# Row-wise largest magnitude of an 8192 x 8192 matrix: 25 tail loads over an 18-row run, and the first load in eight transfers

## The chip, the cores and the metric

The kernel runs on one core of one Trainium2 chip. The metric is the device time of one execution in microseconds (us), the median of several runs. All stretches and instants below are from one profiled execution, and count from the start of its span.

## The reference

```python
def setup_inputs():
    return {
        "x": np.random.randn(8192, 8192).astype(np.float32),
    }

def reference(x: np.ndarray) -> np.ndarray:
    return np.linalg.norm(x, ord=np.inf, axis=1)
```

For a matrix and axis 1 this is the largest absolute value of each row: 268 MB are read, 32 KB are written, and each element is looked at once.

## The kernel before

**Layout.** SBUF holds one ring of 3 x 16384 float32 columns on 128 partitions (`RING`), and behind it a few columns more (`PAD`). Every load goes into the ring by a DMA that SyncE (SP) issues. `Pieces.room` gives out the ring's columns in turn and starts over when a load doesn't fit in what is left. VectorE (DVE) reduces each landed load by `tensor_reduce` with maximum and absolute value, to one column for each matrix row in it.

**The big part.** The first 8192 - 14 x 128 = 6400 rows are taken in 25 loads of two rows a partition: 128 x 16384 columns, 64 KB a partition, 8.389 MB each. In load t, partition p takes rows 256t + 2p and 256t + 2p + 1. One reduction a load writes two results a partition into `res_big`. When all are there, two TensorE transposes and two ScalarE copies turn them into `line`, of 25 rows, which one output DMA stores.

**The tail.** The last 14 x 128 rows (`ROWS = 14`) are laid out as one run of 14 matrix rows, 14 x 8192 columns, on each partition. `tail_loads` cuts this run into 23 loads, worked out from the end backwards: the last has 1344 columns (`FIRST`), and each one before it is as large as the cost of reducing and loading what follows allows. `LOAD` and `REDUCE` are the costs that it reckons with (us a column and us for each operation). `SNAP` moves a cut onto the start of a matrix row when it comes near one, `GRAIN` rounds sizes.

**Combining.** A row of the tail that lies in several loads has a partial result for each; GpSimd (POOL) takes the maximum of these (`tensor_scalar`, L207) into `res_tail`. The last row is treated in another way: its partial results stand directly behind the columns of the last load (`RING + k`), so that the last reduction takes them along. For that it waits until the reduction just ahead of it has written the last of them.

**Order and waits.** Each load has one of 8 semaphores (`SEMS`) in turn. A reduction waits for its load's semaphore; the further reductions of a load that spans several rows keep program order. SP issues all loads in program order from one queue. A load waits for the reductions that read the ring columns it overwrites, and for the reduction of the load 8 before it. The output DMA of `line` (L216) is issued after all input loads; the output of `res_tail`, after the last reduction (L220), ends the kernel.

The lines of the profile that matter: L82 the loads, L100 the reductions, L207 the combinations on POOL, L216 and L220 the two output DMAs.

Of the kernel before, what the change touches and what calls it, by code (L numbers as in the profile page):

```python
# [8 lines left out]
P = 128  # L9
R = 2  # L10
RING = 3 * 16384
PAD = 16
SEMS = 8


LOAD = (1.1775e-3, 0.075)
REDUCE = (1.0417e-3, 0.060)
ROWS = 14
FIRST = 1344
SNAP = 0.5  # L20
GRAIN = 64


def tail_loads(n_cols, big):

    slack = 0.0
    lag = REDUCE[0] * FIRST + REDUCE[1]
    loads = []
    left = ROWS * n_cols
    while left:
        room = lag + slack
        w = FIRST if not loads else 0
        n = 0
        while not w or (loads and n):

            n += 1
            start = (left - 1) // n_cols * n_cols - (n - 1) * n_cols
            fit = int((room - REDUCE[1] * n) / REDUCE[0])
            w = max(w, min(fit, left - start) // GRAIN * GRAIN)
            if fit <= left - start or start <= 0:
                break
        w = max(GRAIN, min(w, big, left))
        row = (left - w + n_cols - 1) // n_cols * n_cols
        if loads and left - row >= SNAP * w:
            w = left - row  # L50
        n = (left - 1) // n_cols - (left - w) // n_cols + 1
        slack += (LOAD[0] - REDUCE[0]) * w + LOAD[1] - REDUCE[1] * n
        loads.append(w)
        left -= w
    return loads[::-1]


class Pieces:
# [7 lines left out]
    def __init__(self, tc, ring):  # L66
        self.tc, self.nc, self.ring, self.head = tc, tc.nc, ring, 0
        self.sems = [tc.alloc_semaphore(f"loaded{i}") for i in range(SEMS)]
        self.started = self.reduced = 0
        self.last = []  # L70

    def room(self, w):
        if self.head + w > RING:
            self.head = 0
        at = self.head
        self.head += w
        return at

    def load(self, at, w, src):
        i = self.started  # L80
        self.started += 1
        ins = self.nc.sync.dma_start(out=self.ring[:, at : at + w], in_=src)  # L82
        ins.then_inc(self.sems[i % SEMS], 16)
        self.tc.no_tile_sem_insts.add(ins.ins.name)
        self.tc.declare_no_dep(ins.ins, group="loads", reason="a reduction stands in between")
        self.tc.add_to_no_dep_group("loads", ins.ins)
        if i >= SEMS:
            self.tc.add_manual_dep(
                ins.ins,
                self.last[i - SEMS].name,  # L90
                mybir.DependencyInfo(mybir.DependencyClass.Sync, mybir.DependencyReason.DATA),
                reason="the semaphore counts one load at a time",
            )

    def reduce(self, pairs):

        i = self.reduced
        self.reduced += 1
        for k, (dst, src) in enumerate(pairs):
            ins = self.nc.vector.tensor_reduce(  # L100
                out=dst,
                in_=src,
                axis=mybir.AxisListType.X,
                op=mybir.AluOpType.max,
                apply_absolute_value=True,
            )
            if k:
                self.tc.keep_in_program_order(ins)
            else:
                ins.wait_op(self.sems[i % SEMS], 16 * (i // SEMS + 1), "sem-ge")  # L110
            self.tc.declare_no_dep(ins.ins, group="loads", reason="waits on the load's semaphore")
        self.last.append(ins.ins)
        return ins


@with_exitstack
def kernel(
    ctx: ExitStack,
    tc: tile.TileContext,
    x: bass.AP,  # L120
    out: bass.AP,
):
    nc = tc.nc
    f32 = mybir.dt.float32
    n_rows, n_cols = x.shape

    tail = tail_loads(n_cols, R * n_cols)
    split = n_rows - ROWS * P
    n_big = split // (R * P)

    x_big = x[:split].rearrange("(t p r) m -> t p (r m)", p=P, r=R)
    x_tail = x[split:].rearrange("(p r) m -> p (r m)", p=P)

    single = ctx.enter_context(tc.tile_pool(name="single", bufs=1))
    psum_pool = ctx.enter_context(
        tc.tile_pool(name="psum", bufs=1, space=bass.MemoryType.PSUM)
    )
    ring = single.tile([P, RING + PAD], f32)  # L140
    ident = single.tile([P, P], f32)
    res_big = single.tile([P, n_big, R], f32)
    res_tail = single.tile([P, ROWS], f32)
    make_identity(nc, ident)
    pieces = Pieces(tc, ring)

    for t in range(n_big):
        at = pieces.room(R * n_cols)
        pieces.load(at, R * n_cols, x_big[t])
        buf = ring[:, at : at + R * n_cols]  # L150
        pieces.reduce([(res_big[:, t, :], buf.rearrange("p (r m) -> p r m", r=R))])


    line = single.tile([n_big, P, R], f32)
    for r in range(R):
        ps = psum_pool.tile([n_big, P], f32, name=f"ps{r}")
        nc.tensor.transpose(ps, res_big[:, :, r], ident)  # L157
        nc.scalar.copy(out=line[:, :, r], in_=ps)  # L158


    parts = []
    col = 0
    for i, w in enumerate(tail):
        c = 0
        while c < w:
            row = (col + c) // n_cols
            n = min(w - c, (row + 1) * n_cols - col - c)
            parts.append((row, i, c, n))
            c += n
        col += w  # L170
    of_row = [[q for q in parts if q[0] == row] for row in range(ROWS)]


    behind = len(of_row[-1]) - 1
    dst = {}
    for row, own in enumerate(of_row):
        if row == ROWS - 1:
            for k, q in enumerate(own[:-1]):
                dst[q] = ring[:, RING + k : RING + k + 1]
            dst[own[-1]] = res_tail[:, row : row + 1]  # L180
        elif len(own) == 1:
            dst[own[0]] = res_tail[:, row : row + 1]
        else:
            some = single.tile([P, len(own)], f32, name=f"parts{row}")
            for k, q in enumerate(own):
                dst[q] = some[:, k : k + 1]
    col = 0
    for i, w in enumerate(tail):
        final = i == len(tail) - 1
        at = RING - w if final else pieces.room(w)  # L190
        pieces.load(at, w, x_tail[:, col : col + w])
        col += w
        own = [q for q in parts if q[1] == i]
        done = pieces.reduce(
            [
                (dst[q], ring[:, at + q[2] : at + q[2] + q[3] + (behind if q == parts[-1] else 0)])
                for q in own
            ]
        )
        for row in range(ROWS - 1):  # L200
            if len(of_row[row]) > 1 and of_row[row][-1][1] == i:
                best = dst[of_row[row][0]]
                more = [dst[q] for q in of_row[row][1:]]
                while more:
                    two, more = more[:2], more[2:]
                    to = best if more else res_tail[:, row : row + 1]
                    nc.gpsimd.tensor_scalar(  # L207
                        out=to,
                        in0=best,
                        scalar1=two[0],  # L210
                        scalar2=two[1] if len(two) == 2 else None,
                        op0=mybir.AluOpType.max,
                        **(dict(op1=mybir.AluOpType.max) if len(two) == 2 else {}),
                    )
    tc.declare_fence(done.ins, group="loads")
    nc.sync.dma_start(  # L216
        out=out[:split].rearrange("(t q) -> t q", q=P * R),
        in_=line.rearrange("t p r -> t (p r)"),
    )
    nc.sync.dma_start(out=out[split:].rearrange("(p r) -> p r", p=P), in_=res_tail)  # L220
# [1 line left out]
_INS = ['x']  # L222
_OUTS = [((8192,), 'float32')]
# [25 lines left out]
```

## Time and profile before

| what | value |
|---|---|
| median of 3 runs | 630.21 us (629.86 to 630.43) |
| profiled execution | 629.88 us |
| its span | 628.0 us |
| VectorE busy | 551.6 us, 88% |
| DMA queue q1 | 268.47 MB in 7086 packets, 428 GB/s over the span |
| one reduction of 128x16384 | 17.22 us |
| one reduction of 128x8192 | 8.675 us |
| reduction of the last load (128x1348) | 1.557 us |
| first load, issue to landing | 21.9 us |
| later big loads, issue to landing | 40.8 us (median) |

The span is the time in which the program's instructions run; the execution's own time has 1.88 us around it. "Issue to landing" counts the time that a load stands in the queue behind others, and so says little on how long its bytes take; for that one compares landings. [...]The DMA share of a stretch counts packets by the moment at which they start, so that short stretches show bursts over 1.

### The profile page before, as it was taken

How to read it: one execution, taken by the hardware profiler on the slowest of the kernel's cores; microseconds unless marked ns; L12 is line 12 of the kernel's file. 1: busy time of each engine (PE TensorE's matmuls, PEld its weight loads, DVE VectorE, ACT ScalarE, POOL GpSimd, SP SyncE). 2: the span in 40 equal slices, each digit the busy share in tenths (PEclk: the TensorE clock that was granted, in tenths of full speed). 3: DMA queues.
4: the chain of work that ended last, by engine and by line, in shares of the span. 5: the costliest groups of instructions: out<-in, count | busy, mean ns of one | idle time of the engine just before them, and what ended most of it. 6: DMA issues, size and time to landing. Idle time of an engine off the chain costs nothing.

```text
span 628.0 us, 165 instructions
## 1 busy us (share of the span) xinstructions
PE 0.6 (0%) x2; PEld 0.2 (0%) x2; DVE 551.6 (88%) x51; ACT 1.8 (0%) x3; POOL 2.5 (0%) x12
## 2 busy tenths in 40 slices
PE   0000000000000000000000000000000000000000
PEld 0000000000000000000000000000000000000000
DVE  0588988889988889888898888998888999999998
ACT  0000000000000000000000000000000000000000
POOL 0000000000000000000000000000000000000000
DMA  9999999999999999999999999999999999999996
GB/s 401 405 463 401 468 401 468 401 468 401 468 401 468 401 468 401 468 401 468 401 468 401 468 401 468 401 468 401 468 401 434 434 430 434 413 434 433 426 424 281
DMA packets 7086, 268.47 MB, mean 428 GB/s; under 512 B 917, under 2 KB 942, under 8 KB 1582
## 3 DMA queue, kind: packets, MB, share of 16 engines
q1 hardware_dynamic: 7086, 268.47, 99.1%
HBM read 268.44 MB, written 0.03 MB: 428 GB/s over the span
## 4 chain that ended last, share of the span: by engine, by line
DMA 55%; DVE 44%; issue 0%; DVEq 0%
DMA ring<-in_x_dram 55%; DVE res_big L100 25%; DVE res_tail L100 10%; DVE parts L100 8%; DVE ring L100 1%; DVEq L100 0%
## 5 line engine op out<-in xcount | busy, mean ns | idle before, releaser
L100 DVE TENSOR_REDUCE res_big<-ring 128x2 f32<-128x16384 f32 x25 | 430.5, 17220 | 73.8 <-DMA ring<-in_x_dram 73.8
L100 DVE TENSOR_REDUCE res_tail<-ring 128x1 f32<-128x8192 f32 (+1 forms) x8 | 61.8, 7785 | 0.1
L100 DVE TENSOR_REDUCE parts<-ring 128x1 f32<-128x384 f32 (+13 forms) x14 | 52.1, 3799 | 0.0
L100 DVE TENSOR_REDUCE ring<-ring 128x1 f32<-128x1728 f32 (+2 forms) x4 | 7.5, 1925 | 0.0
L207 POOL TENSOR_SCALAR res_tail<-parts 128x1 f32<-128x1 f32 x6 | 1.8, 305 | 613.9 <-DVE parts L100 613.9
L158 ACT COPY line<-ps 25x128 f32<-25x128 f32 x2 | 0.5, 262 | 502.9 <-PE ps L157 502.9
L158 ACT ACT_TABLE_LOAD x1 | 1.3, 1283 | 0.7 <-PEq L233 0.7
L157 PE MATMUL ps<-ident,res_big 128*25 128x128 f32 x2 | 0.6, 399 | 504.5 <-DVE res_big L100 504.5
masks.py:199 POOL TENSOR_SCALAR_AFFINE_SELECT ident<-ident 128x128 f32<-128x128 f32 x1 | 0.3, 292 | 0.1
L157 PEld LDWEIGHTS ps<-ident,res_big 128*25 128x25 f32 x2 | 0.2, 123 | 504.4 <-issue 504.4
masks.py:197 POOL MEMSET ident<- 128x128 f32 x1 | 0.2, 204 | 0.3 <-POOLq L233 0.3
L233 POOL MEMSET const-bfloat16-1.0<- 128x1 bf16 x1 | 0.1, 102 | 0.0
L233 POOL MEMSET const-uint8-127<- 128x1 uint8 x1 | 0.1, 101 | 0.0
L233 POOL MEMSET const-float32-0.0<- 128x1 f32 x1 | 0.1, 98 | 0.2 <-issue 0.2
L233 POOL MEMSET const-float32-1.0<- 128x1 f32 x1 | 0.1, 98 | 0.0
## 6 DMA issues: line engine op xcount, KB each, us to landing
ring<-in_x_dram SPq DMA_DIRECT2D x6, 4096.0 KB, 35.9
ring<-in_x_dram SPq DMA_DIRECT2D x1, 4288.0 KB, 34.0
ring<-in_x_dram SPq DMA_DIRECT2D x1, 3904.0 KB, 42.9
ring<-in_x_dram SPq DMA_DIRECT2D x1, 3200.0 KB, 38.8
ring<-in_x_dram SPq DMA_DIRECT2D x1, 2848.0 KB, 45.2
ring<-in_x_dram SPq DMA_DIRECT2D x1, 2272.0 KB, 38.8
ring<-in_x_dram SPq DMA_DIRECT2D x1, 2144.0 KB, 39.8
ring<-in_x_dram SPq DMA_DIRECT2D x1, 2112.0 KB, 42.0
```

Source lines behind the costliest of these rows:

```text
L100: ins = self.nc.vector.tensor_reduce(out=dst, in_=src, axis=mybir.AxisListType.X, op=mybir.AluOpType.max, apply_absolute_value=True,)
L157: nc.tensor.transpose(ps, res_big[:, :, r], ident)
L158: nc.scalar.copy(out=line[:, :, r], in_=ps)
L207: nc.gpsimd.tensor_scalar(out=to, in0=best, scalar1=two[0], scalar2=two[1] if len(two) == 2 else None, op0=mybir.AluOpType.max, **(dict(op ...
L233: nc = _bacc.Bacc("TRN2", target_bir_lowering=False, num_devices=1)
```

## The change

- The tail's run has 18 matrix rows a partition instead of 14, and is cut into 25 loads instead of 23. Two big loads fewer are left (23), so the number of loads is 48 as before.
- `tail_loads` gives a start and a size for each load. The sizes come from the same costs, with `FIRST = 1152` and `SNAP = 0.7`. The very last load is still the end of the last row. The last but one is now the end of the row before it (1280 columns), and the four other pieces of the last row come ahead of that.
- The last load has columns of its own behind the ring (`APART`), with the partial results of its row behind them.
- The first load is issued as eight transfers of 16 partitions: transfer k takes partitions k, k + 8, ..., k + 120, and all eight count on the same semaphore. The first reduction waits for 8 x 16.
- Before the last output DMA, SP waits for POOL in a no-op of its own; the DMA then waits for VectorE only.

The loads of the tail in order, in columns:

```
before  8192 x6, 8576, 7808, 4288, 6400, 5696, 4224, 4544, 4032, 3584, 3008, 2752, 2432,
        1728, 1920, 1728, 1472, 1344
after   16384, 9600, 14976, 12736, 11840, 8192 x3, 5888, 6976, 6208, 5504, 3776, 4416, 3328,
        3520, 3072, 2752, 2432, 1984, 1920, 1664, 1472, 1280, 1152
```

The core of the diff:

```diff
-PAD = 16
+APART = 2048
-ROWS = 14
-FIRST = 1344
-SNAP = 0.5
+ROWS = 18
+FIRST = 1152
+SNAP = 0.7
...
+    ends = [take(end, end - n_cols, FIRST), take(end - n_cols, end - 2 * n_cols, n_cols)]
+    for top, bottom in zip(ends, (end - n_cols, 0)):
+        while top > bottom:
+            top = take(top, bottom, big)
     return loads[::-1]
...
-        ins = self.nc.sync.dma_start(out=self.ring[:, at : at + w], in_=src)
-        ins.then_inc(self.sems[i % SEMS], 16)
...
+        pairs = [(self.ring[:, at : at + w], src)]
+        if i == 0:
+            dst, src = (v.rearrange("(j k) c -> j k c", k=8) for v in pairs[0])
+            pairs = [(dst[:, k], src[:, k]) for k in range(8)]
+        for to, of in pairs:
+            ins = self.nc.sync.dma_start(out=to, in_=of)
+            ins.then_inc(self.sems[i % SEMS], 16)
+            self.counts[i % SEMS] += 16
...
+        self.due.append(self.counts[i % SEMS])
...
-                ins.wait_op(self.sems[i % SEMS], 16 * (i // SEMS + 1), "sem-ge")
+                ins.wait_op(self.sems[i % SEMS], self.due[i], "sem-ge")
...
+            spots[own[-1][1]] = at
+            at += own[-1][3]
+            for q in own[:-1]:
+                dst[q] = ring[:, at : at + 1]
+                at += 1
+            behind[own[-1]] = len(own) - 1
...
-        at = RING - w if final else pieces.room(w)
+        at = spots[i] if i in spots else pieces.room(w)
...
-    nc.sync.dma_start(out=out[split:].rearrange("(p r) -> p r", p=P), in_=res_tail)
+    seen = nc.sync.keepalive_nop([nc.sync.lower_ap(res_tail[:, ROWS - 2 : ROWS - 1])])
+    tc.keep_in_program_order(seen)
+    tc.no_tile_sem_insts.add(seen.ins.name)
+    tc.add_to_no_dep_group("seen", seen.ins)
+    last = nc.sync.dma_start(out=out[split:].rearrange("(p r) -> p r", p=P), in_=res_tail)
+    tc.declare_no_dep(last.ins, group="combined", reason="SyncE has waited for GpSimd")
+    tc.declare_fence(last.ins, group="seen")
```

`take(top, bottom, most)` cuts one load of at most `most` columns off the end of the columns from `bottom` to `top`, and returns where it starts.

## The prediction

> **What bounds the kernel now.** I read the page's busy times first, then the chain of waits, then the timeline of the end, then busy time by stretch. VectorE (DVE) is busy 88% of the span, yet the DMA row of the slices is full to the last but one: the stream of loads sets the time.
>
> ```profile
> PE 0.6 (0%) x2; PEld 0.2 (0%) x2; DVE 551.6 (88%) x51; ACT 1.8 (0%) x3; POOL 2.5 (0%) x12
> DMA  9999999999999999999999999999999999999996
> HBM read 268.44 MB, written 0.03 MB: 428 GB/s over the span
> ```
>
> The chain (start, length, what) says which one ends last where. Up to 487 every step is a load; then VectorE alone carries it.
>
> ```profile
> 0.72 21.94 DMA ring<-in_x_dram
> 22.68 17.23 DVE res_big L100
> 39.93 40.76 DMA ring<-in_x_dram
> ...
> 504.32 60.15 DVE res_tail L100 x7
> 564.47 52.04 DVE parts L100 x14
> 616.51 7.38 DVE ring L100 x4
> 623.89 0.03 issue
> 623.92 0.02 DVEq L100
> 623.94 0.05 issue
> 623.99 1.56 DVE res_tail L100
> ```
>
> The first big reduction starts at 22.68, the 25th at 487.10: (487.10 - 22.68)/24 = 19.35 us a load of 8.389 MB, or 433.5 GB/s, against 17.22 of reducing. So each microsecond by which the first load lands later moves everything behind it by as much.
>
> The start is the one stretch where the stream isn't full (columns: stretch, its length, busy of each engine, clock, DMA share, GB/s by when packets start):
>
> ```profile
> 0.00:1.73 1.73, 0.00 (x0) 0.00 (x0) 0.00 (x0) 1.01 (x1) 0.68 (x6) 1.00 0.00 0
> 1.73:2.10 0.37, 0.00 (x0) 0.00 (x0) 0.00 (x0) 0.27 (x1) 0.00 (x0) 1.00 5.80 1948
> 2.10:2.90 0.80, 0.00 (x0) 0.00 (x0) 0.00 (x0) 0.00 (x0) 0.00 (x0) 1.00 1.02 410
> 2.90:4.80 1.90, 0.00 (x0) 0.00 (x0) 0.00 (x0) 0.00 (x0) 0.00 (x0) 1.00 0.00 0
> 4.80:5.40 0.60, 0.00 (x0) 0.00 (x0) 0.00 (x0) 0.00 (x0) 0.00 (x0) 1.00 4.03 1748
> ```
>
> 1948 x 0.37 and 410 x 0.80 make 0.72 and 0.33 MB: 11 and 5 packets of 65,536 B, one for each of the 16 DMA engines, started over 1.17 us. Their second packets start between 4.8 and 5.4. At full rate a round of 16 takes 1.049 MB / 433.5 GB/s = 2.42 us, so the last engine could have been ready at 1.73 + 2.42 = 4.15 and was at 5.4: at most 1.25 us lies there.
>
> At the end the last load is issued at 607.82 (timeline of SP) and lands 15.9 later, at 623.7; its reduction starts at 623.99. The 0.27 between is VectorE's: busy until 623.89, then 0.10 for the wait on the reduction just before, whose result the last one reads.
>
> [...]reductions with no wait between them overlap by 0.08 us (one of 8192 lasts 8.675, seven take 60.15), and the one that waits for its neighbour starts 0.10 after it.
>
> **The change, part by part.**
>
> *First load.* Transfer k holds partitions k, k+8, ..., k+120. [...]38.5 us instead of 19.35: **+19.2**. [...]Below, nothing excludes 0[...]. Above, 2 x 19.35 gives +19.35.
>
> Nothing covers it: DVE has nothing before the first landing, and loads 2 and 3 are queued behind. Ring space can't give it back, since load 4 waits for the first reduction.
>
> *Start of the stream.* 16 descriptors in the first transfer instead of 128 may bring the engines in sooner: between 0 and -1.25. [...]I take **-0.2**.
>
> *Issues.* SP issues at 0.72, 1.16 and 1.63 before, some 0.45 apart; seven more move the second big load's issue from 1.16 to about 4.3, under a first load that lasts past 22: nothing. Each transfer also ends in a semaphore write. Between 487.08 (landing) and 623.7, 23 loads of 114,688 columns take 136.6 us; with 19.35 for 16384 that is 1.1765 ns a column and 0.073 us a load. The 0.073 holds its packets too, and these stay 128; seven times between 0 and 0.073 is 0 to +0.51: **+0.1**.
>
> *Tail.* 25 + 23 loads become 23 + 25, of the same bytes: the stream is as long as before. Reductions cost 1.0418 ns a column (8.675 for 8192 against 0.541 for 384) and start 0.06 further apart than that (60.15 / 7 = 8.593). Followed load by load from the last big landings, with the old start: VectorE waits 1.75 at the load of 14976 and is never idle again; the last three land at 620.68, 622.26 and 623.69 and start at 620.82, 622.41, 623.81. The ring never holds the stream up: every tail load is issued at least 13 us ahead of its turn. Before, the start was 623.99: -0.18. The new last but one (row 16) stands between the last reduction and the fourth part that it reads, so that wait is met. The last reduction is 1156 columns, not 1348: 192 x 1.0418 = -0.20. Sum **-0.38**; -0.47 if VectorE's lag of 0.10 isn't there, -0.2 if the wait isn't gone.
>
> *Behind it.* Row 16 needs two POOL operations after the reduction of 1280, which ends at 623.89: start 0.1 later as after 616.51 in the trace (616.62), 0.36 + 0.28 and 0.1 between gives 624.75; the last reduction ends at 623.81 + 1.36 = 625.17. So 0.4 of cover; were it gone, the excess would count in full. SP's no-op passes then, and only the output DMA waits for VectorE: before, 0.09 from 625.55 to its issue at 625.64; **-0.04** (0 to -0.07). The 23-row output on one engine: 23 packets of 1 KB[...]; 0.05 each is an upper bound from the 45 packets between 622.81 and 623.23; 1.2 us, done by 625, before the last output's packets. Nine combinations on POOL for six, 0.3 each, spread over the tail: nothing.
>
> Sum: 19.2 - 0.2 + 0.1 - 0.38 - 0.04 = +18.7. The profiled execution (629.88: 628.0 of span and 1.88 around) becomes 648.6; the median of the runs is 0.33 above it: **648.9**.
>
> **The rivals.**
>
> *Engines set the rate[...].* For it: 2.42 us a packet is one engine's pace in the trace[...]. Then only small terms stay: 0.1 - 0.42 = -0.3 with no gain at the start, 629.9; with 0.6 to 1.2 gained there, 628.7 to 629.3. [...]the first load must then land before 24.
>
> *The pairs come apart.* [...]The loss is then what passes until they part: a quarter to three quarters of 19.2, 635 to 644.
>
> *The tail goes wrong.* VectorE or POOL late at the end (the 0.4 of cover gone, the wait still there) costs 0.2 to 0.8 beside either case: 630 to 631 on top of the first rival. It changes no side unless the first load is free.
>
> **How the numbers follow.** Halved rate 0.66, own range 646.5 to 649.8. Pairs apart 0.05. First rival 0.29: 0.17 without a gain at the start, 0.12 with one. A measurement of this kernel can tell about 0.2%, 1.26 us, from no change; below 628.95 means nearly all of the 1.25 at the start, 0.09. So faster 0.09, same 0.20, slower 0.71. The range goes from 629.2 to 649.8: it leaves out most of the rival's gain at the start and the outer edge of the first case.
>
> **What would show it.** The first big reduction starts at about 41.9 instead of 22.68[...]; from there 19.35 a load as before. At the end no gap ahead of the last reduction, which lasts 1.36; the no-op's wait on POOL is over before it ends. [...]VectorE idle in the last 40 us, or more than 0.15 ahead of the last reduction, makes the tail's sum wrong.

## The result and the profile after

| | before | after |
|---|---|---|
| median | 630.04 us (629.86 to 630.43, 4 runs) | 650.78 us (650.62 to 650.87, 4 runs) |
| profiled execution | 629.88 us | 650.62 us |
| its span | 628.0 us | 648.6 us |

The ratio is 1.0328 with a 95% interval of 1.031 to 1.0346: 20.7 us slower. The prediction was 648.9 us with a range of 629.2 to 649.8. The side is right, and so is the place of the loss, the first load; but the time lies 1.0 us above the range. That the rate would halve was the author's estimate: the trace of before has no load of fewer than 128 partitions.

The page of the kernel after, busy times and slices:

```profile
PE 0.6 (0%) x2; PEld 0.2 (0%) x2; DVE 551.8 (85%) x56; ACT 1.8 (0%) x3; POOL 3.3 (1%) x15
DMA  9989999899999989999999998999999999999997
GB/s 194 243 275 445 396 453 453 388 453 453 412 428 453 453 388 453 453 396 445 453 441 400 453 453 388 453 453 412 428 453 421 424 426 442 420 435 426 423 425 297
HBM read 268.44 MB, written 0.03 MB: 414 GB/s over the span
```

VectorE has as much to do as before (551.8 against 551.6 us). The row to look at is GB/s: the first three slices of 16.2 us are near half of all others. The row above it, the DMA engines' share, doesn't show it: a packet that moves slowly counts as busy for all of its time (a share of 1.00 at 207 GB/s in the last stretch below). Only bytes per time tell a slow transfer from a full one.

The chain of waits of after, its first big steps (start, length, what):

```profile
5.11 38.53 DMA ring<-in_x_dram
43.64 0.02 issue
43.66 17.22 DVE res_big L117
...
80.19 40.79 DMA ring<-in_x_dram
120.97 0.02 issue
121.00 17.23 DVE res_big L117
```

The last of the eight transfers is issued at 5.11 and lands 38.53 later; VectorE starts at 43.66 where it started at 22.68. From there the pattern is that of before: 121.00 - 43.66 is four loads, 19.33 each. So 20.98 us enter once and stay.

The start by stretches (stretch, length, busy of each engine, clock, DMA share, GB/s by when packets start):

```profile
0.00:2.05 2.05, 0.00 (x0) 0.00 (x0) 0.00 (x0) 1.28 (x1) 0.68 (x6) 1.00 0.00 0
2.05:2.52 0.47, 0.00 (x0) 0.00 (x0) 0.00 (x0) 0.00 (x0) 0.00 (x0) 1.00 10.06 2231
2.52:6.40 3.88, 0.00 (x0) 0.00 (x0) 0.00 (x0) 0.00 (x0) 0.00 (x0) 1.00 0.00 0
6.40:7.45 1.05, 0.00 (x0) 0.00 (x0) 0.00 (x0) 0.00 (x0) 0.00 (x0) 1.00 4.87 999
11.50:41.90 30.40, 0.00 (x0) 0.00 (x0) 0.00 (x0) 0.00 (x0) 0.00 (x0) 1.00 1.00 207
```

2231 x 0.47 is 1.05 MB, 16 packets: all 16 engines start their one packet between 2.05 and 2.52, none starts another before 6.40. So 16 engines are at work (their share is 1.00 in the last stretch), each slowly, and they stay in step. Call the 16 packets that start together a round. The last stretch holds six rounds: 30.40 / 6 = 5.07 us each against 2.42 at full rate, 207 GB/s.

The end of after, and the wait that is gone (timeline):

```profile
639.97 3.47 DVE L117 TENSOR_REDUCE ring<-ring 128x1 f32<-128x1664 f32 x2
643.36 1.48 DVE L117 TENSOR_REDUCE parts<-ring 128x1 f32<-128x1280 f32 x1
644.75 1.34 DVE L117 TENSOR_REDUCE res_tail<-ring 128x1 f32<-128x1156 f32 x1
645.01 0.28 POOL L225 TENSOR_SCALAR res_tail<-parts 128x1 f32<-128x1 f32 x1 [8.68 <-DVE parts L117]
646.12 0.36 SPq L244 DMA_DIRECT2D out_dram<-res_tail  x1
```

The reduction of 1280 columns ends at 643.36 + 1.48 = 644.84, and the last one starts at 644.75: 0.09 ahead of that, where in the kernel before it started 0.10 after its neighbour's end. It lasts 1.34 instead of 1.56.

### The profile page after: what moved, and what is told of

Read it like the earlier page. It is cut to its first block, busy times and chain, and to the rows that moved or that the text cites. A ratio compares the mean times of both kernels' runs of the same rounds, so it can differ in the third digit from the quotient of the medians.

```text
span 648.6 us, 181 instructions
## 1 busy us (share of the span) xinstructions
PE 0.6 (0%) x2; PEld 0.2 (0%) x2; DVE 551.8 (85%) x56; ACT 1.8 (0%) x3; POOL 3.3 (1%) x15
## 4 chain that ended last, share of the span: by engine, by line
DMA 55%; DVE 43%; SPq 1%; another core or an unknown queue 0%; issue 0%; DVEq 0%
DMA ring<-in_x_dram 55%; DVE res_big L117 24%; DVE parts L117 10%; DVE res_tail L117 8%; DVE ring L117 1%; SPq L97 1%; DVEq L270 0%
## 5 line engine op out<-in xcount | busy, mean ns | idle before, releaser
L117 DVE TENSOR_REDUCE res_big<-ring 128x2 f32<-128x16384 f32 x23 | 396.1, 17220 | 90.5 <-DMA ring<-in_x_dram 90.5
L117 DVE TENSOR_REDUCE res_tail<-ring 128x1 f32<-128x8192 f32 (+1 forms) x10 | 78.9, 7943 | 2.1 <-DMA ring<-in_x_dram 2.1
L117 DVE TENSOR_REDUCE parts<-ring 128x1 f32<-128x3520 f32 (+17 forms) x19 | 69.8, 3735 | 1.7 <-DMA ring<-in_x_dram 1.7
L117 DVE TENSOR_REDUCE ring<-ring 128x1 f32<-128x1984 f32 (+3 forms) x4 | 7.7, 1975 | 0.0
```

The lines of the kernel that those rows point to most:

```text
L117: ins = self.nc.vector.tensor_reduce(out=dst, in_=src, axis=mybir.AxisListType.X, op=mybir.AluOpType.max, apply_absolute_value=True,)
```

## The experiments

Three explanations of a slow first load were set against each other: the partitions that a transfer goes to; sources 512 KB apart in HBM; small transfers as such. Behind the first stands the author's idea that the DMA engines hold each other up where they write. No trace shows that at work; what the runs can show is the rate for each set of partitions. A fourth question was whether the tail has a share in it.

**The tail alone (whole).** The split of the first load is left out.

```diff
-            dst, src = (v.rearrange("(j k) c -> j k c", k=8) for v in pairs[0])
-            pairs = [(dst[:, k], src[:, k]) for k in range(8)]
+            pass
```

> The kernel after with its first load as one transfer of 128 partitions again: the tail alone. All theories of the loss ([...]sources 512 KB apart in HBM; small transfers as such) put it in the first load, so each expects the first big reduction at 22.7 us and the end 0.4 us ahead of the kernel before: a profiled execution near 629.5 us, a median near 629.7. If the tail itself costs something, the time is above that of before, and the first load then cost less than 20.7 us.

Measured: 629.83 us against 630.26, ratio 0.9994 (0.9986 to 1.0002), profiled execution 629.51. The first big reduction starts at 22.57. The loss isn't in the tail. Its own gain is too small for the runs to tell it from none; it shows in the profile, where the end (timeline) is that of after, 21.0 us earlier.

```profile
622.35 1.47 DVE L116 TENSOR_REDUCE parts<-ring 128x1 f32<-128x1280 f32 x1
623.74 1.35 DVE L116 TENSOR_REDUCE res_tail<-ring 128x1 f32<-128x1156 f32 x1
```

**The first load alone (before_eight).** The kernel before, with after's loop over eight transfers in `load` and after's count for the first reduction's wait.

```diff
...
+            dst, src = (v.rearrange("(j k) c -> j k c", k=8) for v in pairs[0])
+            pairs = [(dst[:, k], src[:, k]) for k in range(8)]
...
```

> The kernel before with only its first load split into the eight transfers of every eighth partition. If the two parts of the change add up: first big reduction near 43.7 us as after, all later steps shifted by 21.0 us, a profiled execution near 650.9 us and 0.3 to 0.4 us above the kernel after. If the tail and the first load act on each other, another distance.

Measured: 651.04 us, 1.0329 (1.0314 to 1.0345); profiled 651.03, which is 0.41 above after. The first big reduction starts at 43.95, so 0.29 of the 0.41 is there before the tail begins; by the medians of the runs the distance is 0.26. The two parts add up to within a few tenths.

**Sources side by side (src_near).**

```diff
-            dst, src = (v.rearrange("(j k) c -> j k c", k=8) for v in pairs[0])
+            dst = pairs[0][0].rearrange("(j k) c -> j k c", k=8)
+            src = pairs[0][1].rearrange("(k j) c -> j k c", k=8)
```

> The kernel after, where transfer k of the first load still goes to partitions k, k+8, ..., k+120, but reads 16 neighbouring pairs of matrix rows (64 KB apart instead of 512 KB). The first 256 results then stand in another order. [...]nothing changes, packets near 5.1 us, first big reduction at 43.7, about 650.8 us. HBM addresses 512 KB apart as the cause: packets near 2.4 us, first reduction near 22.5, about 629.6 us.[...]

Measured: 650.74 us, first big reduction at 43.85, the same stretch of six rounds again 207 GB/s:

```profile
11.50:41.90 30.40, 0.00 (x0) 0.00 (x0) 0.00 (x0) 0.00 (x0) 0.00 (x0) 1.00 1.01 207
```

The distance between the sources in HBM is not the cause. Small transfers as such could still be.

**Destinations side by side (dst_near).**

```diff
-            dst, src = (v.rearrange("(j k) c -> j k c", k=8) for v in pairs[0])
+            dst = pairs[0][0].rearrange("(k j) c -> j k c", k=8)
+            src = pairs[0][1].rearrange("(j k) c -> j k c", k=8)
```

> The kernel after, where transfer k of the first load reads the same rows as after (512 KB apart) but goes to 16 neighbouring partitions, 16k to 16k+15. The first 256 results then stand in another order. [...]packets of 4 x 2.42 = 9.7 us[...]: first big reduction between 80 and 85 us, 687 to 692 us in all. HBM addresses as the cause, or small transfers as such: as after, 43.7 and 650.8 us.

Measured: 684.77 us, 1.0864 (1.0844 to 1.0884). The transfers read the same rows as after; only the partitions are others. The stretch of the last six rounds, and then the first big reduction on the timeline:

```profile
18.00:74.50 56.50, 0.00 (x0) 0.00 (x0) 0.00 (x0) 0.00 (x0) 0.00 (x0) 1.00 0.99 111
```

```profile
77.86 17.22 DVE L118 TENSOR_REDUCE res_big<-ring 128x2 f32<-128x16384 f32 x1 [77.86 <-DMA ring<-in_x_dram]
```

The rate is 111 GB/s, near a quarter, with the share of the 16 engines again full (0.99). So the rate goes with the partitions that a transfer writes: 433.5 GB/s with all 128, 207 with every eighth, 111 with 16 neighbours. By landings, the first transfer at 0.72 + 12.1 = 12.8 and the eighth at 4.1 + 73.7 = 77.8, a round is 65.0 / 7 = 9.29 us. I had expected 9.7 (4 x 2.42) to 10.2 (2 x 5.1), and 687 to 692 us in all. So after's round is 5% longer than two of before, but dst_near's is not longer than two of after (10.1).

**Other sets of 16 partitions (stride2, stride4).** Does the round of 5.07 us belong to after's own set? stride2's 4.66 to 4.83 us a packet and stride4's "something between" are for the case that it does: 2.42 is a packet of before, 2.33 a quarter of one of dst_near (those that start between 9.40 and 11.20 have a share of 5.19 over 1.80 us, 9.34 us each). Which set would bring which was the author's guess.

```diff
-            dst, src = (v.rearrange("(j k) c -> j k c", k=8) for v in pairs[0])
-            pairs = [(dst[:, k], src[:, k]) for k in range(8)]
+            # stride2; stride4 has m=2, k=4
+            dst, src = (v.rearrange("(m j k) c -> j m k c", m=4, k=2) for v in pairs[0])
+            pairs = [(dst[:, m, k], src[:, m, k]) for m in range(4) for k in range(2)]
```

> The kernel after with other sets of 16 partitions in the first load's eight transfers: every second one of a block of 32 (32m + k + 2j). [...]as after, 43.7 and 650.8 us. [...]2 x 2.33 to 2 x 2.42, 4.66 to 4.83 a packet, first big reduction between 40 and 41.5, 647 to 648.6 us.

> As stride2, with every fourth partition of a block of 64 (64m + k + 4j)[...]. [...]packets of 5.10, 43.7 and 650.8 us, as after. If it goes by the step between the partitions instead, something between stride2 and after.[...]

Measured: 650.87 and 650.67 us, first big reductions at 43.97 and 43.86, and over the stretch from 11.50 to 41.90 both 207 GB/s (stride2, then stride4):

```profile
11.50:41.90 30.40, 0.00 (x0) 0.00 (x0) 0.00 (x0) 0.00 (x0) 0.00 (x0) 1.00 1.01 207
11.50:41.90 30.40, 0.00 (x0) 0.00 (x0) 0.00 (x0) 0.00 (x0) 0.00 (x0) 1.00 1.00 207
```

Every second of a block of 32, every fourth of a block of 64 and every eighth of all 128 give the same rate. What these three sets have in common, and 16 neighbours have not, no trace shows.

Why a round takes 5.07 us and not 4.83 (2 x 2.42) stays open, but the rounds of after aren't all alike. Stretches of 1.05 us that each hold the starts of one round, from 16.58, 21.68 and 26.60, have DMA shares of 4.87, 4.70 and 4.87, which is 5.11, 4.94 and 5.11 us a packet. The short round is that of the fifth transfer; no run shows why.

**Fewer partitions, spread over all 128 (fourth, second).**

```diff
-            dst, src = (v.rearrange("(j k) c -> j k c", k=8) for v in pairs[0])
-            pairs = [(dst[:, k], src[:, k]) for k in range(8)]
+            # fourth; second has k=2 and range(2)
+            dst, src = (v.rearrange("(j k) c -> j k c", k=4) for v in pairs[0])
+            pairs = [(dst[:, k], src[:, k]) for k in range(4)]
```

> The kernel after with its first load in four transfers of every fourth partition (32 partitions each[...]). [...]full rate, packets of 2.42 us, first big reduction near 22.3, about 629.3 us. If each engine takes two that follow each other in the transfer (8e + k and 8e + 4 + k)[...]: packets near 5.1, 43.7 and about 650.8 us.

> The kernel after with its first load in two transfers of every second partition (64 partitions each[...]). [...]first big reduction near 22.4, about 629.4 us. Dealt out in runs of four (8e + k, 8e + 2 + k, ...): [...]43.7 and about 650.8 us.

How the engines would share out the partitions, on which these figures rest, was the author's guess. Measured: 630.09 us (0.9998, 0.9988 to 1.0008) and 630.12 us (0.9996, 0.9986 to 1.0006). The rate is back. The four transfers of fourth land between 0.71 + 7.8 = 8.5 and 23.09, so that the last three bring 6.29 MB in 14.6 us, 431 GB/s; the second transfer of second brings 4.19 MB between 0.72 + 12.8 = 13.5 and 23.15, 435 GB/s. A partition step as such does not lower it. But against the 22.57 of whole, the first big reductions start later, not earlier (timelines of fourth, then of second):

```profile
23.11 17.22 DVE L117 TENSOR_REDUCE res_big<-ring 128x2 f32<-128x16384 f32 x1 [23.11 <-DMA ring<-in_x_dram]
```

```profile
23.17 17.22 DVE L117 TENSOR_REDUCE res_big<-ring 128x2 f32<-128x16384 f32 x1 [23.17 <-DMA ring<-in_x_dram]
```

In fourth no packet starts before 2.04, where whole has its first between 1.70 and 2.10 (stretches of whole, then of fourth):

```profile
1.70:2.10 0.40, 0.00 (x0) 0.00 (x0) 0.00 (x0) 0.30 (x1) 0.00 (x0) 1.00 6.26 2130
4.65:5.35 0.70, 0.00 (x0) 0.00 (x0) 0.00 (x0) 0.00 (x0) 0.00 (x0) 1.00 3.45 1498
```

```profile
0.00:2.04 2.04, 0.00 (x0) 0.00 (x0) 0.00 (x0) 1.28 (x1) 0.68 (x6) 1.00 0.00 0
2.04:2.90 0.86, 0.00 (x0) 0.00 (x0) 0.00 (x0) 0.00 (x0) 0.00 (x0) 1.00 3.66 1219
2.90:5.10 2.20, 0.00 (x0) 0.00 (x0) 0.00 (x0) 0.00 (x0) 0.00 (x0) 1.00 0.00 0
5.10:5.90 0.80, 0.00 (x0) 0.00 (x0) 0.00 (x0) 0.00 (x0) 0.00 (x0) 1.00 3.03 1311
```

The first transfer has two packets an engine instead of eight, and yet the second packets start between 5.10 and 5.90 instead of 4.65 to 5.35.

**Eight transfers of all partitions (cols8), and a short first round (cols2).**

```diff
-            dst, src = (v.rearrange("(j k) c -> j k c", k=8) for v in pairs[0])
-            pairs = [(dst[:, k], src[:, k]) for k in range(8)]
+            # cols8; cols2 has cuts = [0, 2048, w]
+            cuts = range(0, w + 1, w // 8)
+            pairs = [(pairs[0][0][:, a:b], pairs[0][1][:, a:b]) for a, b in zip(cuts, cuts[1:])]
```

> The kernel after with its first load in eight transfers of all 128 partitions, 2048 columns each: as many transfers, semaphore writes and issues as after[...]. [...]full rate, first big reduction between 22.4 and 22.8 (22.57 with one transfer, plus up to 7 x 0.073 for the transfers, less what shorter first packets save), 629.4 to 629.9 us. If transfers as such cost: later than 24.

> The kernel after with its first load in two transfers of all 128 partitions, 2048 and 14336 columns. It asks what the slow first round is (3.1 us a packet instead of 2.42 with one transfer): if it goes with the bytes of the first packet, packets of 8 KB shorten it and the first big reduction starts between 21.6 and 22.2, 628.6 to 629.2 us profiled; if it is a fixed delay of the first packet on each engine, 22.5 to 22.7 and 629.5 us, no better than with one transfer.

Measured: cols8 629.90 us (0.9995, 0.9987 to 1.0004), first big reduction at 23.08, 0.51 later than in whole and 0.28 later than I allowed. That is 0.073 for each of seven more transfers, the figure that the prediction took from the tail for a load; but here the packets are eight times as many too, so this is no price of transfers alone. Eight transfers as such are not the cause of 21 us. No run has transfers of 16 partitions at the full rate. So the rival that a transfer with one packet an engine is slow by itself was not tested directly; what speaks against it is dst_near, which with as many packets of the same size took almost twice as long again. cols2: 629.59 us (0.9992, 0.9985 to 0.9998), first big reduction at 22.56, level with whole. So shorter first packets bring nothing, and what the slow first round has is a delay of its own. cols2 is the only one whose interval against before lies below 1, by a hair; its first landing is that of whole, so nothing speaks for more than the tail's gain. whole and cols2 are both ahead of before by about 0.4 to 0.6 us, and I can't tell one from the other.

## Why the prediction was right or wrong

| step | predicted | measured |
|---|---|---|
| first load, halved rate | +19.2 | +21.0 |
| start of the stream | -0.2 | 0.0 |
| seven more transfers | +0.1 | in the 21.0 |
| tail | -0.38 | -0.43 |
| last output's issue | -0.04 | -0.06 |

**The step that failed is the size of the first load's term.** The prediction put the first load at 38.5 us, +19.2, and rested the upper end of its range on "Above, 2 x 19.35 gives +19.35". That the rate would halve, and no more, was an estimate for which the trace of before had no load to show. The landings say otherwise: the first transfer is in at 0.72 + 7.6 = 8.3 and the eighth at 43.64, 35.3 / 7 = 5.04 us a transfer, and 8 x 5.04 = 40.35 instead of 19.35. That is +21.0: 2.09 times, 12.9 GB/s an engine (207 / 16) where in before it has 27.1 (433.5 / 16). A factor of two assumed that nothing is lost beyond the halving. Nothing in the profile of before said so, and a bound from above shouldn't have rested on it.

**The start was a second, small miss.** 43.64 - 40.35 = 3.29 stands ahead of the eight rounds, and 22.66 - 19.35 = 3.31 before: no gain. The reading of "at most 1.25 us lies there" took the late second packets for something that fewer descriptors could cure. In part it held: with one packet an engine, the 16 engines come in closer together, within 0.47 us in after and within 0.37 in dst_near (its stretch below; 2834 x 0.37 is 1.05 MB) against 1.05 in whole.

```profile
1.73:2.10 0.37, 0.00 (x0) 0.00 (x0) 0.00 (x0) 0.27 (x1) 0.00 (x0) 1.00 23.24 2834
```

But where the transfers go to partitions with a step between them, the first is issued in 0.54 to 0.59 us against 0.38, and the first packets start some 0.3 later (about 2.05 in after and fourth, 1.7 in whole); and neither fourth nor cols2 landed its load sooner than whole.

**Rivals.** That engines alone set the rate fell at once: 16 engines were at work at half pace (207 GB/s), and dst_near went to a quarter (111). That the pairs come apart, where of two engines that slow each other one gets ahead, fell too: in after all 16 engines stay in step over eight rounds (in each of the last six their packets start within three slices of 0.76 us), and only the fifth is shorter, by 0.17 us. Nor were fewer engines at work: 16 packets start within 0.47 us.

**The tail was right nearly to the hundredth.** Predicted landings of the last three loads, moved by the 20.98, are 641.66, 643.24 and 644.67; the last one is issued at 630.37 and lands about 644.65. The last reduction was predicted 0.18 earlier for the wait and 0.20 shorter; it starts 0.22 earlier by the shift (644.75 - 623.99 = 20.76) and is 0.21 shorter. VectorE's last wait for a load, 1.75 at the one of 14976, is in the profile as 1.67 on top of the 0.08 by which reductions overlap (timeline of after):

```profile
514.45 1.61 DVE L117 TENSOR_REDUCE parts<-ring 128x1 f32<-128x1408 f32 x1
517.73 7.22 DVE L117 TENSOR_REDUCE parts<-ring 128x1 f32<-128x6784 f32 x1 [1.67 <-DMA ring<-in_x_dram]
```

**Behind it.** POOL ends at 645.29, 0.8 ahead of the last reduction's end at 646.10. I had given it 0.4, since I let both operations of row 16 wait for the reduction of 1280; the first combines three older parts and ran at 635.98, when these were there. SP issues the last output 0.02 after VectorE's end, where it was 0.09 before and 0.05 had been predicted. The output of `line` was hidden, as said: its packets start between 644.08 and 645.07, one after another as from one engine (6.9% of the time of 16), ahead of the last output's issue at 646.12.

Added up: 21.0 - 0.43 - 0.06 = 20.5; the span grew by 20.6 and the profiled execution by 20.74. About 0.1 of the rest stands behind the last output's issue: from there to the span's end it was 2.36 us before and is 2.48 now. The cause of that is not known.

## What to carry to other kernels

Before splitting a transfer by partitions, measure the rate for the very sets of partitions that the pieces write: here a stream of 433 GB/s fell to 207 in transfers of 16 partitions with a step of 2, 4 or 8, and to 111 in transfers of 16 neighbours, while the DMA share stayed full (1.00 and 0.99). Transfers of every second or fourth of all 128 partitions kept the rate (435 and 431), and eight by columns landed within 0.51 us of one whole; but none of these made anything start sooner here. And a bound taken from a rate covers only the conditions under which this rate was measured; for a set of partitions that no trace has, leave room above the plain multiple (2.09 here, not 2).

## What the runs showed of the hardware that I had not expected

- In transfers of every eighth partition a round of 16 packets of 64 KB takes 5.04 to 5.07 us, 4 to 5% more than twice 2.42; the fifth round takes 4.94. In transfers of 16 neighbours it takes 9.29, 4% less than four times 2.42. The cause of neither is known.
- A first transfer to partitions with a step between them is issued in 0.54 to 0.59 us against 0.38, and its first packet starts at about 2.05 (after, fourth) instead of 1.7 (whole). This goes with the partitions and not with the sources: src_near, with neighbouring rows, took 0.56, and dst_near, with neighbouring partitions, 0.39.
- What the slow first round costs doesn't go away with smaller or fewer packets: in cols2 the first packets are an eighth as long, in fourth the first transfer has two an engine instead of eight, and the load lands no earlier than in one transfer. In fourth, 0.3 of its 0.54 us of delay goes with the step between the partitions.
